# A fixed order on every engine, from a list schedule over all instructions, in a hybrid diffusion block

## The chip, the cores and the metric

The kernel runs on one core of one Trainium2 chip. The metric is the device time of one execution in microseconds. The core's engines have queues of their own: TensorE (PE; its weight loads are PEld), VectorE (DVE), ScalarE (ACT), GpSimd (POOL) and SyncE (SP, which here only issues transfers). Each queue is taken in its own order; an instruction whose inputs are not there holds all that stand behind it on the same queue.

## What is computed

Two layers over 256 context tokens and 512 latent tokens of width 1024, all in fp32. Layer 1 updates the latent tokens alone. Cut from the reference:

```python
mod_l = (jax.nn.silu(c) @ mod_w[i] + mod_b[i])[:, None, :]
sh1_l, sc1_l, g1_l, sh2_l, sc2_l, g2_l = jnp.split(mod_l, 6, -1)
p_lat = modulate(x_lat, sh1_l, sc1_l) @ w_in[i]
p_ctx = modulate(x_ctx, sh1_c, sc1_c) @ w_in[i]
y_ctx, y_lat = token_mixers(p_ctx, p_lat, ...)
x_lat = deepnorm_update(x_lat, y_lat @ w_out[i], g1_l, ln1_g[i], ln1_b[i])
m_lat = sq_relu_mlp(modulate(x_lat, sh2_l, sc2_l), w_up[i], w_down[i])
x_lat = deepnorm_update(x_lat, m_lat, g2_l, ln2_g[i], ln2_b[i])
```

The context has its own modulation, made from `c_ctx`, and in layer 0 the same two updates. The mixers, gMLP, grouped attention and gated DeltaNet, stand side by side. The DeltaNet runs in chunks of 64 tokens, forwards and backwards, and each chunk needs the inverse of a triangular matrix.

## The kernel before

**Staging.** A layer has four stages. `mix` first modulates the normed tokens and makes the projections for the gates and the gMLP; then it makes the nine convolution units (`dn_conv`), the queries and keys (`qk_norm`) and the values and `z`, while `dn_prep` works on the DeltaNet's decay matrices for two pairs of heads at a time. In its third part `dn_make` and `dn_scan` run for three pairs of heads beside `attention`. `rest` then multiplies the mixed tokens by `w_out` (`outp`, with `after` for norm and modulation) and calls `mlp`, which goes through the hidden width in eight groups of three to five 128-wide units: the up products of a group, squared ReLU, then the down products, token tile by token tile, into one PSUM tile (`ax`) of 1024 columns each; VectorE adds it to `acc`. Beside layer 0's MLP, `mod_dve` computes the next layer's modulation on VectorE, one step (`acc<-modw,cz,acc`) at each signal `pace`.

**Products.** Weights and activations are split into a high and a low fp32r part (`whi`, `wlo`; the split takes one ScalarE and one VectorE instruction), and each product is three (`mm3`). The DeltaNet's products are 64x64 or 32x32 and use a part of the array, so that two or four run side by side. `Feed` streams weights: `raw` buffers for the load (`wraw`), `parts` buffers for the split halves, five in the MLP.

**The inverse.** `dn_prep` transposes the masked matrix to `Lx` on VectorE, then runs 31 steps of two VectorE instructions (`tm`, then `Xx`), each on the result of the one before, and transposes the result to `PA` and `PB`.

**What sets the order.** `Flow` (line 40 on) runs the stages' generators while the program is written. It keeps a small clock of its own and always continues the one that could start earliest, with `BIAS` 1000 ns in favour of the DeltaNet's chains. It also hands out PSUM: four tiles `mm` of 512 columns and two tiles `ax` of 1024 are lent by name, so which product uses which tile, and in which turn, is fixed by then. The scheduler of the programming layer takes the finished text, in which each instruction has a priority by its place (`AHEAD` moves `dn_prep` 300 places forward), and puts out for each engine the ready instruction of the best priority. Every instruction goes through `_Engine.call`, line 213, which is why the profile puts all of them on L213 and one has to go by tile names. `_body` (line 656) builds and runs the kernel; `K.open` and `K.close` (line 302 on) open and close the SBUF pools, and a tile of a new pool waits for the tiles that lay in its place.

Of the kernel before, what the change touches and what calls it, by code (L numbers as in the profile page):

```python
# [9 lines left out]
F32R = mybir.dt.float32r  # L10
# [3 lines left out]
PSUM = bass.MemoryType.PSUM  # L14
DRAM = bass.MemoryType.DRAM

P = 128
# [22 lines left out]
class Flow:  # L40
# [8 lines left out]
    def __init__(self, tc):  # L49
        self.tc = tc  # L50
        self.free = {}
        self.ready = {}
        self.done = {}
        self.live = []
        self.count = 0
        self.last = 0.0
        self.slots = {}
        self.spare = {}
        self.lent = {}
# [7 lines left out]
    @staticmethod  # L67
    def width(a):
        n = 1
        for s in a.shape[1:]:  # L70
            n *= s
        return n
# [150 lines left out]
            setattr(self, k, _Engine(flow, k, getattr(nc, k)))  # L223


def _tb(v):

    return 1 - v if v < 2 else 7 - v
# [62 lines left out]
class K:  # L291
    def __init__(self, ctx, tc, d, dump=None):
        self.tc = tc
        self.flow = Flow(tc)
        self.nc = _Core(tc.nc, self.flow)
        self.d = d
        self.dump = dump
        self.ctx = ctx
        self.open_ = []


    def open(self, name, side="left", space=None):
        kw = {} if space is None else {"space": space}
        cm = self.tc.tile_pool(name=name, bufs=1, side=side, reuse_waits="tile", **kw)
        p = cm.__enter__()
        self.open_.append((p, cm))
        return p

    def close(self, *pools):
        for p in pools:  # L310
            i = next(i for i, (q, _) in enumerate(self.open_) if q is p)
            self.open_.pop(i)[1].__exit__(None, None, None)

    def setup(self):
        nc, tc, ctx, d = self.nc, self.tc, self.ctx, self.d
# [340 lines left out]
def _body(ctx, tc, d, out, dump=None, stop=None):  # L656
    K_ = Kernel(ctx, tc, d, dump)
    K_.run(out, stop)
    for p, cm in reversed(K_.open_):
        cm.__exit__(None, None, None)  # L660

# [17 lines left out]
class Kernel(K):  # L679
# [784 lines left out]
    def dn_make(self, l, p, v, qkv, G, A, TT, r):  # L1464
# [5 lines left out]
        kds, ks, egc, be, E = G["kds"], G["ks"], G["egc"], G["be"], G["E"]  # L1470
        hs = slice(2 * p, 2 * p + 2)
        td = (v, _tb(v))
        a0 = 0 if l == 0 else 2
        he = lambda a: a.rearrange("p t (h e) -> p t h e", e=HD)
# [59 lines left out]
    def dn_scan(self, l, p, v, A, r, S, o):  # L1534

        nc, sc = self.nc, self.dn
        need = l == 0 or v > 1
        a0 = 0 if l == 0 else 2
        td = (v, _tb(v))
        mm = nc.tensor.matmul  # L1540
        halves = [_half(f) for f in range(2)]
# [405 lines left out]
```

## Time and profile before

| | us |
|---|---|
| median of 3 runs | 2045.34 |
| lowest and highest | 2045.0, 2048.18 |
| the profiled execution | 2041.46 |
| its span, first to last instruction | 2039.7 |
| mean granted TensorE clock (1 is full speed) | 0.949 |

A page of the profile gives the busy time of each engine, a view of stretches gives the same for any part of the span, a view of waits tells how long an engine stood idle and whose instruction ended that, and a timeline lists instructions by their start, equal neighbours merged. In rows of the timeline and of groups, `out<-in` are tile names without buffer numbers, then shapes; in a group, `x80 | 101.0, 1280 | 8.5` is the count, the busy us, the mean ns of one, and the idle us of the engine just before them. TensorE's matmuls overlap in the pipeline, so the duration of one is longer than its share.

### The profile page before, as it was taken

How to read it: one execution, taken by the hardware profiler on the slowest of the kernel's cores; microseconds unless marked ns; L12 is line 12 of the kernel's file. 1: busy time of each engine (PE TensorE's matmuls, PEld its weight loads, DVE VectorE, ACT ScalarE, POOL GpSimd, SP SyncE). 2: the span in 40 equal slices, each digit the busy share in tenths (PEclk: the TensorE clock that was granted, in tenths of full speed). 3: DMA queues.
4: the chain of work that ended last, by engine and by line, in shares of the span. 5: the costliest groups of instructions: out<-in, count | busy, mean ns of one | idle time of the engine just before them, and what ended most of it. 6: DMA issues, size and time to landing. Idle time of an engine off the chain costs nothing.

```text
span 2039.7 us, 35034 instructions
## 1 busy us (share of the span) xinstructions
PE 1859.0 (91%) x14424; PEld 1508.4 (74%) x14424; DVE 1280.2 (63%) x2159; ACT 854.6 (42%) x1607; POOL 283.8 (14%) x479
## 2 busy tenths in 40 slices
PE   6999887888898999999999979988878879999997
PEld 2788665666678878887888777877667668788886
DVE  4668786856688154544555866879785585444555
ACT  3434434467546322331232174543655554323331
POOL 1111215531021000000000121121522020000001
PEclk8999898989999999999999979987998989999999
DMA  7211016213327223333453333110000554222331
GB/s 280 91 63 49 27 45 216 76 38 111 118 96 232 86 90 118 114 114 92 156 165 106 102 136 99 53 37 20 20 27 19 176 184 136 83 83 84 113 105 50
DMA packets 79172, 204.49 MB, mean 100 GB/s; under 512 B 15854, under 2 KB 30062, under 8 KB 77988
## 3 DMA queue, kind: packets, MB, share of 16 engines
q1 hardware_dynamic: 67876, 184.56, 28.0%
q10 hardware_dynamic: 11136, 17.70, 2.3%
q8 instruction: 113, 1.85, 0.4%
q14 instruction: 47, 0.39, 0.1%
HBM read 184.41 MB, written 17.82 MB: 99 GB/s over the span
## 4 chain that ended last, share of the span: by engine, by line
PE 61%; DVE 19%; issue 7%; ACT 5%; POOL 4%; DMA 4%; SPq 0%; ACTq 0%; POOLq 0%; DVEq 0%
PE mm L213 36%; PE ax L213 25%; DVE cacc L213 2%; DVE wlo L213 2%; DVE tm L213 2%; DVE Xx L213 2%; POOL crn L213 2%; DMA modw<-in_mod_w 1%; DVE M L213 1%; DMA wraw<-in_w_up 1%; POOL rs L213 1%; DVE st L213 1%; DMA wraw<-in_w_out 1%; ACT ape L213 1%; DVE anm L213 1%
## 5 line engine op out<-in xcount | busy, mean ns | idle before, releaser
L213 DVE TENSOR_TENSOR wlo<-wraw,whi 128x1024 fp32r<-128x1024 f32 (+2 forms) x188 | 226.5, 1211 | 254.8 <-ACT whi L213 254.4
L213 ACT ACTIVATE whi<-wraw 128x1024 fp32r<-128x1024 f32 (+2 forms) x188 | 194.5, 1049 | 450.7 <-PE ax L213 287.9
L213 PE MATMUL mm<-x2xh,whi 128*128 128x256 f32 (+1 forms) x832 | 287.8, 346 | 12.4 <-ACT whi L213 11.4
L213 PE MATMUL mm<-x2xh,wlo 128*128 128x256 f32 (+1 forms) x832 | 286.6, 345 | 1.0 <-DVE wlo L213 1.0
L213 PE MATMUL mm<-x2xl,whi 128*128 128x256 f32 (+1 forms) x832 | 287.0, 345 | 0.0
L213 PE MATMUL ax<-whi,hh 128*128 128x512 f32 x640 | 251.3, 393 | 0.0
L213 PE MATMUL ax<-whi,hl 128*128 128x512 f32 x640 | 249.6, 391 | 0.0
L213 PE MATMUL ax<-wlo,hh 128*128 128x512 f32 x640 | 249.5, 390 | 0.0
L213 PEld LDWEIGHTS mm<-x2xh,whi 128*128 128x128 f32 x832 | 158.6, 191 | 36.1 <-ACT whi L213 12.1
L213 PEld LDWEIGHTS mm<-x2xh,wlo 128*128 128x128 f32 x832 | 158.5, 191 | 22.3 <-DVE wlo L213 1.5
L213 PEld LDWEIGHTS mm<-x2xl,whi 128*128 128x128 f32 x832 | 158.8, 191 | 21.1 <-issue 0.8
L213 DVE TENSOR_TENSOR acc<-acc,ax 128x1024 f32<-128x1024 f32 x68 | 82.9, 1219 | 144.0 <-PE ax L213 144.0
L213 PEld LDWEIGHTS ax<-whi,hh 128*128 128x128 f32 x640 | 120.1, 188 | 33.7 <-ACT hh L213 6.1
L213 PEld LDWEIGHTS ax<-whi,hl 128*128 128x128 f32 x640 | 120.1, 188 | 30.7 <-issue 4.2
L213 PEld LDWEIGHTS ax<-wlo,hh 128*128 128x128 f32 x640 | 120.2, 188 | 26.3 <-issue 1.7
L213 POOL TENSOR_SCALAR rs<-mv 128x1 f32<-128x1 f32 x52 | 32.9, 632 | 702.7 <-DVE mv L213 701.5
L213 DVE SCALAR_TENSOR_TENSOR acc<-modw,cz,acc 128x1024 f32<-128x1024 f32 x80 | 101.0, 1280 | 8.5 <-DMA modw<-in_mod_w 4.4
L213 ACT ACTIVATE rl<-mm 128x256 f32<-128x256 f32 (+1 forms) x104 | 51.0, 491 | 131.5 <-PE mm L213 131.3
L213 POOL MEMSET acc<- 128x1024 f32 x10 | 9.5, 954 | 477.1 <-PE mm L213 477.1
L213 ACT ACTIVATE v<-mm,sh,sc 128x128 f32<-128x128 f32 x152 | 58.3, 462 | 29.4 <-PE mm L213 25.2
L213 DVE SCALAR_TENSOR_TENSOR cacc<-cb,cw,cacc 128x772 f32<-128x772 f32 (+1 forms) x72 | 69.9, 973 | 0.7 <-ACT cacc L213 0.2
L213 DVE TENSOR_REDUCE anm<-ax 128x1 f32<-128x768 f32 (+1 forms) x60 | 50.5, 847 | 31.3 <-PE ax L213 30.9
(255 smaller groups left out, 4104.0 us busy)
## 6 DMA issues: line engine op xcount, KB each, us to landing
modw<-in_mod_w SPq DMA_DIRECT2D x64, 512.0 KB
wraw<-in_w_up SPq DMA_DIRECT2D x64, 512.0 KB
wraw<-in_w_down SPq DMA_DIRECT2D x64, 512.0 KB
wraw<-in_w_ch SPq DMA_DIRECT2D x22, 512.0 KB
modw<-in_mod_w SPq DMA_DIRECT2D x32, 256.0 KB
modw<-in_mod_w SPq DMA_DIRECT2D x8, 1024.0 KB
wraw<-in_w_out SPq DMA_DIRECT2D x16, 512.0 KB
x_d<-xt ACTq DMA_DIRECT2D x16, 512.0 KB
```

The lines of the kernel that those rows point to most:

```text
L213: return f(*args, **kw)
```

## The change

After the program text is written, a new class `Order` reads all its instructions. `graph` finds the data dependences from the memory that each one reads and writes, keeps users of one PSUM tile in turn, and adds the waits that come from reused SBUF (for which `Pools` records when pools open and close). `costs` gives each instruction a duration from its kind, width and engine. `units` joins neighbouring products that use different parts of the array, when their kinds (the names of their tiles) agree. `tail` works out the longest chain of costs behind each instruction, and `schedule` simulates the five engines and one DMA bus: whichever engine is free first takes, of what is ready, the instruction with the longest chain. On TensorE, among the first 16, one of the same kind as the last counts as 5000 ns longer, and a part of the array that is still busy counts against. `apply` ties each instruction to the one before it on its engine, for order only. No instruction is added or altered. The core of the diff:

```diff
+class Order:
+    SAME, OTHER = 110.0, 220.0
+    LOOK, STICK, LATE, SWITCH = 16, 5000.0, 20.0, 250.0
...
+    def costs(self):
...
+            if kind == "InstDMACopy":
+                o = x.outs[0].bass_ap
+                self.moved[-1] = 4 * math.prod(int(c) for _, c in o.ap)
+                c = 330.0 if eng == E.SP else 60.0
+            elif kind == "InstMatmult":
+                n = width(x.outs[0])
+                m = width(x.ins[1])
+                if x.ins[1].dtype == F32R:
+                    c = max(35.0 + 0.58 * m, 0.4175 * n + 13.0)
+                else:
+                    c = (1.0 if x.is_transpose else 2.0) * max(0.42 * m, 0.835 * n + 2.0)
...
+            elif eng == E.DVE:
...
+                c = 70.0 + (50.0 * vec if n > 1 else 40.0) + n * (1.9 if kind == "InstStreamTranspose" else 0.53 if fast else 1.04)
+            elif eng == E.Activation:
+                c = 100.0 + 0.82 * n + (100.0 if len(x.outs) > 1 else 0.0) + (170.0 if vec > 1 else 0.0)
...
+    def units(self):
+        pe = [i for i in range(self.n) if self.cells[i]]
...
+            self.kind[i] = tuple(a.bass_ap.tensor.name.split("_")[0].rstrip("0123456789") for a in (*x.ins, *x.outs) if hasattr(a, "bass_ap"))
+            part = len(self.cells[i]) < 16
+            if unit and (not part or used & set(self.cells[i]) or any(newest(j) > unit[0] and j not in unit for j in self.pred[i]) or self.kind[i] != self.kind[unit[0]]):
+                close()
+                unit, used = [], set()
...
+    def tail(self):
...
+        for i in reversed(order):
+            c = self.dur[i] + (2200.0 + self.moved[i] / 340.0 if self.moved[i] else 0.0) if i < self.n else 0.0
+            far[i] = c + max((far[j] + self.lag(i, j) for j in succ[i]), default=0.0)
...
+    def schedule(self, key):
...
+            elif e == E.PE:
+                some = [heapq.heappop(avail[e]) for _ in range(min(len(avail[e]), self.LOOK))]
+                worth = lambda c: (c[0] - self.STICK * (self.kind[c[1]] == last) + self.LATE * max(0.0, max(cell[q] for q in self.cells[c[1]]) - t), c[1])
+                pick = min(some, key=worth)
...
+                i = pick[1]
+                queue = [k for k in self.unit.get(i, ()) if k != i]
+            else:
+                k, i = heapq.heappop(avail[e])
+            t = max(t, ready[i])
+            if self.cells[i]:
+                t = max([t] + [cell[c] + (self.SWITCH if kinds[c] != self.kind[i] and not self.round[i] else 0.0) for c in self.cells[i]])
...
+    def apply(self):
+        far = self.tail()
+        out = self.schedule([-f for f in far])
+        dep = mybir.DependencyInfo(mybir.DependencyClass.NoSync, mybir.DependencyReason.DATA)
+        for e, seq in out.items():
+            for a, b in zip(seq, seq[1:]):
+                self.tc.add_manual_dep(self.ins[b], self.ins[a].name, dep)
...
     def open(self, name, side="left", space=None):
         kw = {} if space is None else {"space": space}
         cm = self.tc.tile_pool(name=name, bufs=1, side=side, reuse_waits="tile", **kw)
-        p = cm.__enter__()
+        p = _Pool(self.pools, cm.__enter__(), side)
...
 def _body(ctx, tc, d, out, dump=None, stop=None):
     K_ = Kernel(ctx, tc, d, dump)
     K_.run(out, stop)
+    Order(tc, K_.pools).apply()
```

## Rows read from the trace of the kernel before

**Rows 1.** Head of the page: span; busy us, share, instructions by engine.

```profile
span 2039.7 us, 35034 instructions
...
PE 1859.0 (91%) x14424; PEld 1508.4 (74%) x14424; DVE 1280.2 (63%) x2159; ACT 854.6 (42%) x1607; POOL 283.8 (14%) x479
```

**Rows 2.** Stretches: length; PE, PEld, DVE, ACT, POOL busy us; clock; DMA share; GB/s.

```profile
0.00:55.00 55.00, 35.20 (x130) 14.46 (x130) 25.69 (x66) 22.38 (x37) 5.64 (x18) 0.88 0.80 281
55.00:305.00 250.00, 226.94 (x1589) 191.48 (x1589) 187.53 (x399) 104.62 (x166) 42.62 (x48) 0.93 0.16 51
305.00:460.00 155.00, 127.70 (x2842) 96.58 (x2840) 101.65 (x276) 81.83 (x242) 69.98 (x153) 0.90 0.33 110
460.00:640.00 180.00, 156.85 (x1048) 126.64 (x1049) 126.22 (x194) 105.10 (x234) 25.82 (x32) 0.97 0.38 129
640.00:1174.00 534.00, 534.00 (x2673) 439.15 (x2671) 284.44 (x267) 149.41 (x199) 15.82 (x20) 1.00 0.38 119
1174.00:1430.00 256.00, 224.43 (x1560) 189.62 (x1558) 199.02 (x425) 127.96 (x222) 51.99 (x70) 0.87 0.22 69
1430.00:1580.00 150.00, 123.50 (x2498) 101.12 (x2500) 102.42 (x256) 87.96 (x223) 50.27 (x110) 0.87 0.07 22
1580.00:1680.00 100.00, 80.92 (x530) 64.75 (x526) 69.09 (x102) 53.57 (x118) 14.30 (x22) 0.95 0.51 175
1680.00:2022.00 342.00, 341.99 (x1540) 278.79 (x1539) 173.61 (x168) 121.78 (x172) 3.67 (x4) 1.00 0.30 95
```

**Rows 3.** TensorE's waits over the whole span: us in total, times, longest.

```profile
PE mm L213 <- ACT whi L213: 20.2, 8, 5.6
PE mm L213 <- DVE axn L213: 12.9, 6, 4.6
...
PE ax L213 <- DVE PB L213: 10.1, 5, 2.7
PE mm L213 <- DVE wlo L213: 9.6, 12, 2.3
```

**Rows 4.** Two inverse runs, stretches of `tm` steps alone; then VectorE's timeline.

```profile
168.45:228.02 59.57, 21.00 (x62) 0.96 0.12 36
257.24:297.85 40.61, 21.02 (x62) 0.96 0.14 46
...
201.45 1.02 DVE L213 SCALAR_TENSOR_TENSOR cacc<-cb,cw,cacc 128x772 f32<-128x772 f32 x1
```

**Rows 5.** A group of the page; VectorE's timeline in layer 0's MLP.

```profile
L213 DVE SCALAR_TENSOR_TENSOR acc<-modw,cz,acc 128x1024 f32<-128x1024 f32 x80 | 101.0, 1280 | 8.5 <-DMA modw<-in_mod_w 4.4
...
857.38 1.22 DVE L213 TENSOR_TENSOR acc<-acc,ax 128x1024 f32<-128x1024 f32 x1
858.52 4.86 DVE L213 SCALAR_TENSOR_TENSOR acc<-modw,cz,acc 128x1024 f32<-128x1024 f32 x4
863.31 1.21 DVE L213 TENSOR_TENSOR acc<-acc,ax 128x1024 f32<-128x1024 f32 x1
```

**Rows 6.** Timeline of the kernel's end.

```profile
2029.04 0.39 PE L213 MATMUL ax<-whi,hl 128*128 128x512 f32 x1
2029.46 1.22 DVE L213 TENSOR_TENSOR acc<-acc,ax 128x1024 f32<-128x1024 f32 x1 [0.69 <-PE ax L213]
...
2034.29 1.28 DVE L213 SCALAR_TENSOR_TENSOR xt<-xt,rstd,lb 128x1024 f32<-128x1024 f32 x1 [0.72 <-POOL rstd L213]
```

**Rows 7.** The group of table loads on ScalarE, then ScalarE's timeline around one.

```profile
L213 ACT ACT_TABLE_LOAD x13 | 16.7, 1283 | 5.4 <-DVE gc L213 4.5 <-PEq L1939 0.7
...
1211.70 1.19 ACT L213 ACTIVATE xmxh<-v 128x512 fp32r<-128x512 f32 x2
1212.91 1.28 ACT L213 ACT_TABLE_LOAD   x1
1214.20 0.21 ACT L213 ACTIVATE ea<-ea 128x12 f32<-128x12 f32 x1
```

**Rows 8.** TensorE's timeline in layer 0's DeltaNet stage.

```profile
348.10 1.04 PE L213 MATMUL mm<-kv,TT 64*64 64x128 f32 x15
```

More of the change, by code (lines that the diff above doesn't have):

```diff
@@ new lines, with __init__, size, tile @@
+class Pools:
+    def __init__(self):
+        self.events = []
+class _Pool:
+    def __init__(self, pools, pool, side):
+        self.pools, self.pool, self.side, self.tags = pools, pool, side, {}
+        pools.events.append(("open", self))
+    def size(self):
+        return sum(b * n for b, n, _ in self.tags.values())
+    def tile(self, shape, dtype, tag=None, bufs=1, name=None):
+        kw = {} if tag is None else {"tag": tag}
+        t = self.pool.tile(shape, dtype, bufs=bufs, name=name, **kw)
+        tag = tag or name
+        n = 4 * math.prod(shape[1:])
+        n = -(-n // 32) * 32
+        b, k, names = self.tags.get(tag, (0, 0, []))
+        names.append(t.tensor.name if hasattr(t, "tensor") else t.name)
+        self.tags[tag] = max(b, n), max(k, bufs), names
+        return t
@@ L299, in __init__ @@
         self.open_ = []
+        self.pools = Pools()
     def open(self, name, side="left", space=None):
@@ L312, in close @@
             self.open_.pop(i)[1].__exit__(None, None, None)
+            self.pools.events.append(("close", p))
     def setup(self):
```

296 lines of the change are left out of this document (added).

## The prediction, made blind

> **What bounds the kernel now.** I read the head of the page first, then the stretches of busy time, then TensorE's own waits, and last single stretches of the timeline. The head [rows 1] has TensorE busy for 1859.0 of 2039.7 us, so 181 us are idle and no other engine is near its limit (VectorE 1280.2). The stretches [rows 2] show that this is an average over two kinds of stage. In the two MLP stages (640 to 1174 and 1680 to 2022) TensorE is busy for 534.0 of 534 and 341.99 of 342 us at a granted clock of 1.00: no order of instructions makes these 876 us shorter, it can only make them longer. In the stages of projections, DeltaNet, attention and output projection TensorE idles for 23.1 us (55:305), 27.3 (305:460), 23.2 (460:640), 31.6 (1174:1430), 26.5 (1430:1580) and 19.1 (1580:1680), in sum 150.8 us, and its clock is down: 0.87 to 0.97. Of the rest of the idle time 19.8 us lie in the first stretch, where the DMA engines move 281 GB/s, and the last 10 us behind the last product. No engine fills a mixed stage: the busiest, TensorE apart, is VectorE with 199.02 of 256 us in 1174:1430. So these stages are bound by chains that go from engine to engine, and by the order in which each engine takes their links.
>
> **What the change is, as the trace sees it.** No instruction is added, removed or altered; there is no new semaphore. What is new is that each of the five queues, SP's and POOL's included, gets one fixed order, from a list schedule whose priority is the longest chain of modelled costs behind an instruction. The order before came out of the same data dependences too, with the order of the program text as its priority. Two things stay frozen. Flow still hands out the six PSUM tiles (`mm0` to `mm3`, `ax0`, `ax1`) by name while the program is written, and users of one PSUM tile keep their order. And the SBUF pools keep their places, so a tile of a later stage still waits for those that lay there. What can change is how six chains of PSUM users are threaded against each other, and what VectorE, ScalarE, POOL and the DMA queues do first.
>
> **First term: waits that the order makes.** By what ended them, TensorE waited [rows 3] 20.2 us for `whi` and 9.6 for `wlo` (weights split late on ScalarE and VectorE), 12.9 for `axn` (normalised queries and keys) and 10.1 for `PB` (the end of the triangular inverse). I count these four as made by the order: these producers had their inputs earlier and stood behind other work. The inverse shows it best: its first run takes 59.6 us from `Lx` to `PA`, but its 62 `tm` and `Xx` steps take 21.0 us of VectorE [rows 4]; convolution taps of 1.02 us, such as the one at 201.45, stand between its steps. The next run takes 40.6 us for the same work. A priority by the longest chain puts these steps first. The rest of the idle time I leave to the data. So 20.2 + 9.6 + 12.9 + 10.1 = 52.8 us are the order's own, and I take 50 of the 150.8 us; the bounds are 0 (the same chains wait elsewhere) and 150.8.
>
> **Second term: the clock.** The chip grants one of two levels, 1.2 or 2.4 GHz, so a mean of 0.87 over 256 us says that 2 x 0.13 x 256 = 67 us ran at the lower one; over the six mixed stretches it is 35 + 31 + 11 + 67 + 39 + 10 = 193 us [rows 2], in which work took twice its time: at most 96 us. The level is low in stretches where TensorE idles between products and at 1.00 where it doesn't. With a third of the idle gone I take 10 us; the bounds are 96 and, if the new order spreads the products more thinly, -20.
>
> **Third term: what the MLP stages lose.** The schedule prefers, by 5000 ns of priority, a product of the same kind as the last one. In the MLP's second half two token tiles have their `ax` tile free at once, with equal chains behind them. So products of two token tiles will alternate and both tiles will end together. Now they go one after the other: the sums `acc<-acc,ax` on VectorE come 5.9 us apart (857.38, 863.31) and take 1.21 to 1.22 each, behind the next tile's products [rows 5]. Paired, both `ax` tiles are full at one moment, and TensorE needs other work for 1.22 us of sum and some 0.4 us of hand-over (an estimate: the last product begins at 2029.04 and the sum at 2029.46 [rows 6], and the way back to TensorE is of the same kind, each less the product's own run). There are 3 x 8 such ends in layer 0 and 2 x 8 in layer 1, 40 in all; the bounds are 0 and 40 x 1.6 = 64 us. Up products of the next group cover some of them, but the five buffers of `whi`/`wlo` hold four down units, which leaves one unit of cover in each group. I count one bare end in each of 16 groups, less some 40% as pairs fall out of step after the first: 16 x 1.6 x 0.6 = 15 us lost.
>
> **Fourth term: stage ends.** Paired tiles also end together before a norm. At the end of the kernel the last tile goes from its sum at 2029.46 to the end of its second scaling at 2034.29 + 1.28 in 6.1 us [rows 6]; another tile's share may come in front of it. The end of each of the two output projections is alike. I take 10 us in all, between 0 and 3 x 6.1 = 18.
>
> **Fifth term: ScalarE's tables.** There are 13 table loads of 1.283 us now, 16.7 us [rows 7], in the two stretches where Gelu stands beside Exp and Tanh. `Order.costs` prices an activation by its width alone, so nothing in the new order keeps the functions together. Up to 13 more would be 17 us of ScalarE, and in 1174:1430 it has 128 of 256 us to hide them in; I take 4, between 0 and 17. The Trainium skill ("ScalarE: Activation LUTs", What ACT_TABLE_LOAD costs) gives 2.66 us for each change of set, 1.283 of load and some 1.38 of drain; by that price the bound would be 35 us. The trace [rows 7] agrees on the load but shows no drain: the activation before ends at 1212.89, the load runs from 1212.91, and the next activation begins at 1214.20.
>
> **The queues.** SP issues loads as buffers come free; a load put ahead of its turn holds the loads behind it. I cost that at nothing in the MLP stages, where DMA is busy for 0.30 to 0.38, and include it in the bounds of the first term elsewhere. VectorE's modulation sums (`acc<-modw`, 80 of 1.280 us, 101.0 us [rows 5]) were paced by hand beside the MLP; now they fill any gap there. That costs nothing as long as an `ax` sum has 5 us to spare, and 1.28 us or more for an end of a pair that meets one.
>
> **The sum.** The profiled execution took 2041.46 us: a span of 2039.7 and 1.8 around it. 2041.5 - 50 - 10 + 15 + 10 + 4 = 2010.5. It lies 3.9 us under the median of the runs shown, 2045.34, so I forecast a median of 2014.4, 1.5% faster. The case's own range is 1980 to 2040.
>
> **The rivals.** *The chains gain more.* If two thirds of the idle time go (100 us) with 30 us of clock, and the pairs cost 10: 2041.5 - 120 + 3.9 = 1925. For it: VectorE's 102 of 155 and 102 of 150 us in the DeltaNet stages leave room for that. Against: there TensorE is busy for 128 and 124 us, mostly with small products that keep their order in PSUM.
> *The pairs cost more than the chains gain: slower.* The place is the second half of the MLP. A pair that ends while modulation sums run waits behind them; now up to four come in a row, 4.86 us [rows 5]. With two of them (2.56 us) ahead of a sum the 24 ends of layer 0 cost 4.2 us each, those of layer 1 1.6, in sum 126; two thirds of that is 83. With 25 us gained by the first term and 14 lost by the fourth and fifth: 2041.5 + 83 - 25 + 14 + 3.9 = 2117. Against the first two terms as forecast it decides from (50 + 10 - 14) / 40 = 1.2 us of idle TensorE at each of the 40 ends. For it: TensorE has no slack there at all. Against: sums now have priority over modulation where their chain is longer, and up products fill.
> *The mixed stages lose.* The preference for the same kind holds a step of the scan back behind a run such as the 15 `kv` products of 1.04 us [rows 8], by half of it if the step comes due anywhere in the run. The 72 steps of the scans (2 layers, 3 pairs of heads, 6 tiles, 2 halves) would then cost 72 x 0.52 = 37 us: 2041.5 + 37 - 25 + 14 + 3.9 = 2071, slower. It decides from 0.15 us a step.
> *It does next to nothing.* PSUM tiles handed out beforehand and the frozen pools leave the order much as it was: within 4 us of 2045.
>
> **How the numbers follow.** A measurement of this kernel tells about 0.2%, 4 us, from no change. The forecast has 0.43, more from the chains 0.12, the pairs 0.26, the mixed stages 0.11, no change 0.08. Faster is 0.55, the same 0.08, slower 0.37. Both signs hold much of the chance, so the range is wide: from 1940, which leaves out the better half of the first rival, to 2105, which takes in the pairs up to 12 us under their centre.
>
> **What would show it.** Right: the first inverse run well under 59.6 us, `whi` and `wlo` together under half of 29.8 us in TensorE's waits, the granted clock of 1174:1430 above 0.87. Third term: any idle TensorE in the MLP stages, ended by `acc` on VectorE; none would refute it. Fifth: the number of table loads beside 13. The forecast is wrong if TensorE's idle time outside the MLP stays at 150 us, or if the MLP stages grow by more than 50.

## The result, and the profile after

| | before | after |
|---|---|---|
| median | 2046.76 | 2065.39 |
| lowest and highest of 4 | 2045.0, 2051.8 | 2064.6, 2066.6 |
| profiled execution, its span | 2041.46, 2039.7 | 2066.6, 2064.8 |
| mean granted clock | 0.949 | 0.948 |

All times are in us. The ratio of after to before is 1.0087 with a 95% interval of 1.0068 to 1.0107: the changed kernel is 0.9% slower, where I had forecast 1.5% faster (2014.4 us). The first and second fence answer to [rows 1] and [rows 2]: the head of the page, then stretches of the span, cut where the stages end in the changed kernel (length; busy us of PE, PEld, DVE, ACT, POOL; clock; DMA share; GB/s).

```profile
span 2064.8 us, 35099 instructions
...
PE 1871.9 (91%) x14424; PEld 1515.1 (73%) x14424; DVE 1283.9 (62%) x2159; ACT 842.2 (41%) x1605; POOL 293.1 (14%) x479
```

```profile
55.00:278.00 223.00, 215.24 (x1496) 182.96 (x1495) 182.26 (x384) 99.54 (x157) 45.39 (x47) 0.98 0.18 59
278.00:463.00 185.00, 140.85 (x3008) 108.58 (x3006) 115.69 (x302) 91.15 (x258) 70.73 (x155) 0.88 0.26 87
463.00:640.00 177.00, 159.08 (x967) 124.94 (x968) 116.17 (x178) 96.59 (x219) 22.31 (x30) 0.94 0.34 117
640.00:1174.00 534.00, 526.75 (x2674) 439.15 (x2673) 280.01 (x266) 146.33 (x207) 12.73 (x18) 0.99 0.38 123
1174.00:1409.00 235.00, 210.82 (x1401) 179.64 (x1399) 184.03 (x377) 116.17 (x203) 51.68 (x56) 0.89 0.23 75
1409.00:1591.00 182.00, 151.08 (x2754) 117.69 (x2754) 134.12 (x322) 100.56 (x249) 62.25 (x129) 0.90 0.07 22
1591.00:1684.00 93.00, 68.37 (x368) 53.50 (x366) 56.87 (x83) 41.34 (x88) 13.06 (x18) 0.89 0.46 160
```

The first line is layer 0's projections: they end at 278 where they ended at 307.7, TensorE is idle for 7.8 us of them and its clock is 0.98 (0.93 in 55:305 before). The second line is the DeltaNet stage, with 44.2 us idle of 185; in 305:460 before it was 27.3 of 155. The six lines without the MLP (the fourth) leave 7.8 + 44.2 + 17.9 + 24.2 + 30.9 + 24.6 = 149.6 us idle, against 150.8 before: the idle time moved, and none of it went.

A table by stage shows where to. A stage's border is the end of its last product in the trace; "head" is the time from layer 0's last down product to layer 1's first convolution product, "out-projection" reaches from the last attention product to the first up product, with the gaps at both ends. Times are for the profiled executions; columns 4 to 7 are experiments below.

| stage | before | after | proj_only | no_switch | proj_mix | proj_nosw |
|---|---|---|---|---|---|---|
| L0 projections | 307.7 | 278.2 | 277.6 | 277.5 | 279.4 | 278.4 |
| L0 DeltaNet, attention | 224.2 | 256.2 | 235.1 | 236.1 | 256.6 | 235.4 |
| L0 out-projection | 85.1 | 78.3 | 85.1 | 77.8 | 84.7 | 85.1 |
| L0 MLP | 557.8 | 564.3 | 557.6 | 558.7 | 557.9 | 560.9 |
| head of L1 | 42.5 | 46.8 | 41.1 | 47.2 | 42.1 | 43.2 |
| L1 projections | 202.8 | 185.3 | 185.0 | 187.7 | 185.6 | 187.5 |
| L1 DeltaNet, attention | 186.3 | 201.5 | 199.7 | 198.6 | 201.7 | 200.5 |
| L1 out-projection | 59.4 | 74.1 | 60.9 | 71.0 | 63.1 | 60.8 |
| L1 MLP | 363.6 | 366.9 | 363.8 | 365.8 | 363.3 | 363.5 |
| tail | 10.3 | 13.2 | 9.9 | 13.2 | 9.9 | 9.9 |
| span | 2039.7 | 2064.8 | 2015.9 | 2033.6 | 2044.3 | 2025.2 |

From before to after the two projection stages win 29.5 + 17.5 = 47 us. The two DeltaNet and attention stages lose 32.0 + 15.2 = 47 us, as much. The rest, +6.5 and +3.3 in the MLPs, +4.3, +14.7 and +2.9 at the stage ends and -6.8 in layer 0's out-projection, is the 25 us by which the span grew.

These two 47 us are in part one and the same: work has crossed the border. Before, the second inverse of layer 0 was done in time for its 192 small products (96 of `PB,M`, 48 each of `PA,zs` and `zs,PA`) to run ahead of the last projection product; in the changed kernel and in the four experiments of the table they stand behind it. So a second border is of use, the first `kv` product, with which `dn_make` begins (times in us):

| | before | after | proj_only | no_switch | proj_mix | proj_nosw |
|---|---|---|---|---|---|---|
| L0, last projection to first `kv` | 8.0 | 21.1 | 18.9 | 18.8 | 21.1 | 18.8 |
| L0, first `kv` to last attention product | 216.2 | 235.1 | 216.2 | 217.3 | 235.5 | 216.7 |
| L1, last projection to first `kv` | 2.8 | 1.1 | 2.5 | 1.5 | 1.1 | 1.5 |
| L1, first `kv` to last attention product | 183.4 | 200.4 | 197.2 | 197.1 | 200.6 | 199.0 |

Counted to it, layer 0 gains 16.4 us ahead of it (it comes at 299.3 in place of 315.7) and loses 18.9 behind it; layer 1 gains 19.3, counted from its first convolution product, and loses 17.0.

The inverse did what the first term says. These are the stretches of its first two runs with its `tm` steps alone, as in [rows 4] (length; VectorE's busy us; clock; DMA share; GB/s):

```profile
158.10:200.50 42.40, 21.16 (x62) 0.96 0.15 50
253.50:289.10 35.60, 21.20 (x62) 0.89 0.23 87
```

The first run takes 42.4 us for the same 21 us of steps, where it took 59.6. The second runs from 253.5 to 289.1 where it ran from 257.24 to 297.85 [rows 4], so it ends only 8.8 us earlier, while the projections end 29.5 us earlier. And here are TensorE's waits over the span, to be read beside [rows 3] (us, times, longest):

```profile
PE mm L213 <- ACT whi L213: 19.8, 6, 9.3
...
PE mm L213 <- DVE rP L213: 13.1, 10, 3.0
...
PE mm L213 <- DVE S L213: 10.6, 12, 2.7
...
PE mm L213 <- DVE wlo L213: 7.9, 2, 7.4
...
PE mm L213 <- DVE axn L213: 5.7, 4, 2.3
```

Two of these rows in the kernel before:

```profile
PE mm L213 <- DVE rP L213: 11.5, 12, 2.2
...
PE mm L213 <- DVE S L213: 4.4, 7, 1.1
```

`axn` has more than halved, but `whi` and `wlo` stand at 27.7 us (29.8 before): 9.3 and 7.4 us of that are now single waits, ahead of layer 1's out-projection and in its head. `rP` and `S` are links of the scan: `rP`, third largest before, has grown a little, and `S` has more than doubled.

### The profile page after: what moved, and what is told of

Same layout as the page of the kernel before. It is cut to its first block, busy times and chain, and to the rows that moved or that the text cites. A ratio compares the mean times of both kernels' runs of the same rounds, so it can differ in the third digit from the quotient of the medians.

```text
span 2064.8 us, 35099 instructions
## 1 busy us (share of the span) xinstructions
PE 1871.9 (91%) x14424; PEld 1515.1 (73%) x14424; DVE 1283.9 (62%) x2159; ACT 842.2 (41%) x1605; POOL 293.1 (14%) x479
## 5 line engine op out<-in xcount | busy, mean ns | idle before, releaser
L213 PE MATMUL mm<-x2xh,whi 128*128 128x512 f32 (+1 forms) x832 | 212.1, 349 | 9.3 <-ACT whi L213 4.5
L213 PE MATMUL ax<-whi,hh 128*128 128x512 f32 x640 | 208.9, 395 | 6.4 <-ACT hh L213 3.6
L213 PE MATMUL mm<-x2xl,whi 128*128 128x256 f32 (+1 forms) x832 | 208.8, 346 | 0.0
L213 PE MATMUL mm<-x2xh,wlo 128*128 128x256 f32 (+1 forms) x832 | 207.2, 345 | 0.0
L213 PE MATMUL ax<-wlo,hh 128*128 128x512 f32 x640 | 206.3, 391 | 0.1
L213 PE MATMUL ax<-whi,hl 128*128 128x512 f32 x640 | 202.5, 391 | 0.2 <-DVE hl L213 0.2
L213 PEld LDWEIGHTS mm<-x2xl,whi 128*128 128x128 f32 x832 | 145.9, 192 | 21.1
L213 ACT ACTIVATE rl<-mm 128x512 f32<-128x512 f32 (+1 forms) x104 | 49.2, 495 | 106.6 <-PE mm L213 105.9
L213 DVE TENSOR_TENSOR hl<-rl,hh 128x768 fp32r<-128x768 f32 (+2 forms) x76 | 53.8, 716 | 46.3 <-ACT hh L213 46.1
L213 ACT ACTIVATE v<-mm,sh,sc 128x128 f32<-128x128 f32 x152 | 56.9, 468 | 38.5 <-PE mm L213 31.6
L213 PE MATMUL mm<-whi,yh 128*128 128x512 f32 x160 | 59.0, 405 | 14.9 <-ACT whi L213 11.1
```

The lines of the kernel that those rows point to most:

```text
L213: return f(*args, **kw)
```

## Experiments

Each kernel was timed in three rounds beside the kernel before on the same chip. A stage in what follows is a part of the program text: projections (A), DeltaNet and attention (C), out-projection (D), MLP (E), each with its layer; a list `self.stage` holds the part of each instruction. No experiment leaves out any computation.

### Which stages gain, which lose

Kernel `proj_only`:

```diff
         for e, seq in out.items():
+            seq = [i for i in seq if self.stage[i][0] == "A"]
             for a, b in zip(seq, seq[1:]):
```

> The fixed order is put only on instructions of the projection stages (modulation, gates, gMLP, convolutions, queries, keys, values, of both layers); all others are left to the old scheduler. In the changed kernel layer 0's projections end at 278.2 us where they ended at 307.7 (29.5 earlier), layer 1's take 11 us less, and the DeltaNet and attention stages behind them take 32 and 15 us more. Theory one, the new order inside the DeltaNet stages is what is bad: they go back to 224 and 186 us, the gain of 40 us is kept, 2046.8 - 40 = 2007. Theory two, the DeltaNet stages end when their own chains let them, however early the projections end: 2047, the same as before. A clear loss would say that the new order of the projections itself starts things late (2060 or more).

Measured: 2018.21, ratio 0.9877 (0.9857 to 0.9896). So the new order of the projections alone makes the kernel 1.2% faster than before. It keeps 24 of the 47 us: layer 0's DeltaNet stage takes 235.1 us, 21 less than in the changed kernel, but still 11 more than before, and layer 1's 199.7, about as much as in the changed kernel. Theory one holds for layer 0 to two thirds. The remainder there stands ahead of the first `kv` product, on TensorE's timeline, first in the kernel before and then in `proj_only`:

```profile
301.77 1.71 PE L213 MATMUL ax<-PB,M 32*32 32x32 f32 x96 [1.96 <-DVE PB L213]
...
315.75 2.79 PE L213 MATMUL mm<-kv,TT 64*64 64x128 f32 x22 [8.03 <-DVE kv L213]
```

```profile
290.54 2.77 PE L213 MATMUL ax<-PB,M 32*32 32x32 f32 x96 [12.94 <-DVE PB L213]
...
296.45 1.97 PE L213 MATMUL mm<-kv,TT 64*64 64x128 f32 x16
```

The projections are done at 277.6, and TensorE idles 12.94 us for the end of the second inverse and then runs its products; the kernel before had begun these products at 301.77, ahead of the end of its projections at 307.7, and behind that waited 8.0 us, for `kv`. From the first `kv` product on, the stage takes 216.2 us in both kernels. So layer 0 gains 19.3 us, the first `kv` product's, and keeps all of them; the other 10 of the 29.5 were work behind the border. Layer 1 keeps about 4 of its 17.8 us. There, too, work has crossed: 96 of VectorE's `tm` and `Xx` steps lie behind the projections in place of 62, and its busy time there is 138.3 us in place of 126.3. That this makes the loss is likely, not shown; TensorE's granted clock, 0.85 there in place of 0.90, is another candidate, but it is 0.91 in the changed kernel, whose layer 1 loses as much.

Kernel `no_mixers`, with the same line and the condition `self.stage[i][0] != "C"`:

> The fixed order is put on every stage but the DeltaNet and attention stages, which are left to the old scheduler. In the changed kernel the stages behind attention lose 7.5 us (start of layer 1's output projection), 6 (its end to the first up product), 3.3 (MLP of layer 1), 6.5 (MLP of layer 0) and 2.9 (the tail), less 3.4 won in layer 0's output projection: about 23. Theory one (the order inside the DeltaNet stages is bad): 2007 + 23 = 2030. Theory two (these stages end by their own chains): 2047 + 23 = 2070.

Measured: 2040.13, ratio 0.9972 (0.9955 to 0.9990). That is 22 us above `proj_only`: the new order of the output projections, the MLPs and the tail costs 22 us by itself. In the profiled executions most of the difference lies where it was expected, from layer 0's out-projection on; but 6 us of it lie ahead of that, in layer 0's DeltaNet stage (241.4 us), whose order is left to the old scheduler in both.

### Four suspects in the schedule

Kernel `no_kind`:

```diff
-    LOOK, STICK, LATE, SWITCH = 16, 5000.0, 20.0, 250.0
+    LOOK, STICK, LATE, SWITCH = 16, 0.0, 20.0, 250.0
```

> The changed kernel with the preference for a product of the same kind as the last one set from 5000 ns to 0. Theory A, this preference holds steps of the scan back behind runs of other products and pairs the token tiles in the MLP: DeltaNet stages of 230 and 190 us in place of 256 and 201, and the MLP of layer 0 back at 558 us from 564: 2065 - 26 - 11 - 6 = 2022. Theory B, the loss comes from the longest-chain priority and the transfers' order, not from the preference: 2060 to 2070. It can also be slower, if the runs of one kind saved time in the array's sharing: 2080 or more.

Measured: 2074.71, ratio 1.0154 (1.0133 to 1.0175): 9 us slower than the changed kernel. Layer 0's DeltaNet stage took 270.6 us. The preference for the same kind, which my third rival held guilty, is a gain there. One part of theory A came true: layer 0's MLP took 557.0 us, and layer 1's 360.6, so in these two stages the preference costs 7 and 6 us.

Kernel `sp_free`:

```diff
         for e, seq in out.items():
+            if e == mybir.EngineType.SP:
+                continue
```

> The changed kernel, but SyncE's queue of transfers gets no fixed order; the four computing engines do. In the changed kernel layer 1's output projection starts 9.3 us after the last attention product (1.8 before), because its weights are issued at 1611.19, behind loads of y that wait for attention's last store. Theory T, the transfers' order makes the losses at the stage ends: that gap goes back to about 2 us, the one to the first up product from 13 to 7, the tail from 13 to 10, 16 us in all: 2049. If the transfers' order only follows the rest, nothing changes: 2065.

Measured: 2079.15, ratio 1.0173 (1.0151 to 1.0196): 14 us slower than the changed kernel. The gap ahead of layer 1's output projection did shrink, from 9.3 to 4.0 us, but the other two stayed at 13 us, and both DeltaNet stages took 7 us more. A fixed order on the engines whose loads come in another order costs more than the fixed loads do.

Kernel `no_switch`:

```diff
-    LOOK, STICK, LATE, SWITCH = 16, 5000.0, 20.0, 250.0
+    LOOK, STICK, LATE, SWITCH = 16, 5000.0, 20.0, 0.0
```

> The changed kernel with the price of 250 ns for a product of another kind on the same part of the array set to 0. In the changed kernel the products `id,qd` and `A,rwu`, which alternate in the program by twos on the same two quarters of the array, lie spread out: from the end of `rwu` to the start of `rP` a tile of layer 0 takes 11.0 us in the mean where it took 5.2 before (5.1 with the order on the projections alone), and one run of them 3.4 us in place of 1.1. Theory S, the schedule believes that each change of kind costs 250 ns and puts other products between, which the scan then waits for: without the price 11.0 falls to 6 or less, the DeltaNet stages end some 20 and 10 us earlier, 2065 - 30 = 2035. Theory P, the priority by the longest chain itself is at fault: 2060 to 2070, and the 11 us stay.

Measured: 2036.12, ratio 0.9969 (0.9954 to 0.9984), as theory S expected: 29 us faster than the changed kernel through one constant, 20 of it in layer 0's DeltaNet stage. Layer 1's became only 3 us shorter, where 10 were expected; the rest came from layer 0's MLP and layer 1's out-projection. The time from `rwu` to `rP`, a mean over the 18 tiles of layer 0, fell from 11.0 to 7.3 us, short of the 6 expected. TensorE's waits for the links of the scan in 278:470 show it too, in the changed kernel and then without the price:

```profile
PE mm L213 <- DVE rP L213: 6.8, 6, 3.0
...
PE mm L213 <- DVE S L213: 5.3, 5, 2.7
...
PE mm L213 <- ACT rQ L213: 4.8, 3, 3.4
```

```profile
PE mm L213 <- DVE rP L213: 2.1, 4, 1.2
...
PE mm L213 <- ACT rQ L213: 1.9, 3, 1.3
...
PE mm L213 <- DVE S L213: 1.3, 2, 1.2
```

16.9 us have become 5.3. What the price does in the changed kernel is seen on TensorE's timeline of one tile, one of the slow ones. Its `rwu` was ready at 308.25, and this is the part from the first `id,qd` on:

```profile
323.55 0.27 PE L213 MATMUL mm<-id,qd 64*64 64x64 f32 x2
...
323.93 1.06 PE L213 MATMUL mm<-modw,cz 128*32 128x512 f32 x8
324.93 0.33 PE L213 MATMUL mm<-id,qd 64*64 64x64 f32 x4
...
325.97 0.28 PE L213 MATMUL mm<-A,rwu 64*64 64x64 f32 x4
326.08 0.28 PE L213 MATMUL mm<-id,qd 64*64 64x64 f32 x4
326.20 0.28 PE L213 MATMUL mm<-A,rwu 64*64 64x64 f32 x4
...
327.66 0.33 PE L213 MATMUL mm<-id,qd 64*64 64x64 f32 x4
327.92 1.06 PE L213 MATMUL mm<-modw,cz 128*32 128x512 f32 x8
328.92 0.33 PE L213 MATMUL mm<-A,rwu 64*64 64x64 f32 x4
```

`id,qd` and `A,rwu` alternate on the same two quarters of the array, and between them stand products of the modulation (`modw,cz`, 1.06 us each time) and others, so the run lasts from 323.55 to 329.25. `rP` waits for the end of it and starts at 329.37, 21 us after `rwu`. The run makes 5.7 of these; before it TensorE was at the tile ahead, whose own run lasted from 312.94 to 318.91. In `proj_only` the same kind of run looks like this:

```profile
426.40 0.28 PE L213 MATMUL mm<-id,qd 64*64 64x64 f32 x4
426.52 0.28 PE L213 MATMUL mm<-A,rwu 64*64 64x64 f32 x4
426.64 0.28 PE L213 MATMUL mm<-id,qd 64*64 64x64 f32 x4
...
426.75 0.28 PE L213 MATMUL mm<-A,rwu 64*64 64x64 f32 x4
...
427.22 0.28 PE L213 MATMUL mm<-A,rwu 64*64 64x64 f32 x4
...
427.62 0.42 DVE L213 TENSOR_TENSOR rP<-mm,ei 128x256 f32<-128x256 f32 x1 [0.90 <-PE mm L213]
```

Each change of kind takes 0.11 to 0.12 us, the groups' own run included; the schedule reckons 250 ns on top. By the single records, two products of one kind start 0.058 us apart on the same quarter (426.403 and 426.461), and the first of the next kind follows after 0.059 (426.520). One part of the expectation missed: the runs themselves stayed long, 2.9 us in the median (3.4 in the changed kernel, 1.1 before), so other products still stand in them without the price.

Kernel `any_units`:

```diff
-            if unit and (not part or used & set(self.cells[i]) or any(newest(j) > unit[0] and j not in unit for j in self.pred[i]) or self.kind[i] != self.kind[unit[0]]):
+            if unit and (not part or used & set(self.cells[i]) or any(newest(j) > unit[0] and j not in unit for j in self.pred[i])):
```

> The changed kernel, but neighbouring products that share the array are joined to a unit whatever their kinds. So `kd,rwu` and `rwu,kd`, which use different halves of the array's quarters, go side by side again: before, their 32 records took 0.69 us a tile, in the changed kernel 0.98. If their separation costs the scan its 0.3 us on each of 36 tiles: 2065 - 11 = 2054. If that is covered: 2065. The alternation of `id,qd` and `A,rwu` uses the same quarters and isn't joined by this, so the theory of the 250 ns price expects no more than the 11 us.

Measured: 2088.76, ratio 1.0225 (1.0200 to 1.0250): 23 us slower than the changed kernel, which neither line expected. The 32 records of `kd,rwu` and `rwu,kd` are back at 0.69 us a tile, but the same joining puts the scan's `S,rP` and `S,rQ` into one run (`S,rQ` some 1.6 us a tile in the median in place of some 0.8), and layer 1's DeltaNet stage takes 224.6 us. That the second made the loss is not shown, and one number speaks against it: `S,rQ` took 1.5 us a tile in the kernel before as well, whose DeltaNet stages are the shortest of these three. The cause of this loss stays open.

### The priority, and an order on some engines only

Kernel `text_key`:

```diff
-        out = self.schedule([-f for f in far])
+        out = self.schedule([float(i) for i in range(self.m)])
```

> The changed kernel, but the list schedule's priority is the place in the program text, as before the change, in place of the longest chain; costs, units, preference and the fixed order stay. If the longest-chain priority is at fault in the DeltaNet stages: about 2020 to 2045, and the gain in the projections (29.5 us in layer 0) shrinks too, since that priority made it. If the schedule's prices are at fault, or an order fixed by modelled times as such: 2065 or more, with `rwu` to `rP` still at 8 us or above.

Measured: 2075.65, ratio 1.0167 (1.0137 to 1.0196). The text's order as priority is 10 us worse than the longest chain. In its profiled execution (2083.55) both projection stages are longer (layer 0's end at 291.1, not at 278.2; layer 1's take 196.7 us, not 185.3), layer 0's out-projection too (89.8), while its MLP is shorter (551.3). Layer 0's DeltaNet stage is as slow as in the changed kernel (257.8 us). So the longest chain is not what slows it.

Kernel `mix_nope`:

```diff
         for e, seq in out.items():
+            seq = [i for i in seq if self.stage[i][0] == "A" or self.stage[i][0] == "C" and e != mybir.EngineType.PE]
             for a, b in zip(seq, seq[1:]):
```

> The fixed order on the projections for all engines, and in the DeltaNet and attention stages for all engines but TensorE; the rest is left to the old scheduler. With the projections alone it was 2018.2. If TensorE's order is what makes the DeltaNet stages slow: 2015 to 2022, the same. If VectorE's, ScalarE's, GpSimd's or SyncE's order is: 2018 + 20 + 3 (what the changed kernel loses there in the two layers) = 2041.

Measured: 2087.64, ratio 1.0223 (1.0194 to 1.0252). Layer 0's DeltaNet stage took 287.7 us, more than with either full order. With TensorE in one order and its suppliers in another the question can't be answered; the run shows that the order of one engine has no price of its own.

### Stage ends, and a kernel put together

Kernel `ends_free`, the price at 0 and the condition `self.stage[i] not in ("D1", "E1")`:

> The price of another kind at 0, and the fixed order on everything but the output projection and the MLP of layer 1 with the tail, which are left to the old scheduler. In the kernel without the price these took 11.6 + 2.2 + 2.9 = 16.7 us more than before (last attention product to first up product 71.0 in place of 59.4, MLP 365.8 in place of 363.6, tail 13.2 in place of 10.3). If the order at the stage ends makes that (two token tiles reach their norms together, weights stand behind y loads): 2036 - 17 = 2019. If the lateness comes in from the attention stage before: 2036.

Measured: 2022.65, ratio 0.9887 (0.9869 to 0.9904), 13.5 under `no_switch`. The stretch from the last attention product to the first up product went from 71.0 to 61.0 us, the MLP from 365.8 to 363.6, the tail from 13.3 to 9.9. In the changed kernel the first of these gaps reads as follows, on the queues and on TensorE:

```profile
1608.36 1.74 SPq L213 DMA_DIRECT2D y<-y_d  x2
...
1610.90 0.33 ACTq L213 DMA_DIRECT2D y_d<-ayb  x1
1611.19 5.98 SPq L213 DMA_DIRECT2D wraw<-in_w_out  x3
...
1618.77 1.06 ACT L213 ACTIVATE whi<-wraw 128x1024 fp32r<-128x1024 f32 x1 [3.54 <-DMA wraw<-in_w_out]
...
1619.88 1.22 PE L213 MATMUL mm<-whi,yh 128*128 128x512 f32 x2 [9.31 <-ACT whi L213]
```

The last three weights of the projection are issued at 1611.19, behind loads of `y` that were put ahead of them on SP, and TensorE waits 9.31 us (1.8 in the kernel before). The tail shows the other kind of end, two token tiles together, on VectorE:

```profile
2050.26 1.22 DVE L213 TENSOR_TENSOR acc<-acc,ax 128x1024 f32<-128x1024 f32 x1 [3.29 <-PE ax L213]
...
2052.12 1.20 DVE L213 TENSOR_TENSOR acc<-acc,ax 128x1024 f32<-128x1024 f32 x1
...
2058.45 2.48 DVE L213 SCALAR_TENSOR_TENSOR xt<-xt,rstd,lb 128x1024 f32<-128x1024 f32 x2 [0.71 <-POOL rstd L213]
```

From the last sum at 2052.12 to the end of the second scaling at 2060.93 it takes 8.8 us, where [rows 6] has 6.1 for one tile.

Kernel `best`, the price at 0 and the condition `self.stage[i] in ("A0", "C0", "D0", "A1", "C1")`:

> The price of another kind at 0, and the fixed order on the projections, the DeltaNet and attention stages of both layers and the output projection of layer 0; the two MLPs, layer 1's output projection and the tail are left to the old scheduler. From the stages measured so far: with the order on the projections alone it was 2018.2; layer 0's output projection with its gaps took 77.8 us in place of 85.1 in the kernel without the price. So 2018 - 7 = 2011, if stages add up. If the change of order at a border between the two schedulers costs something, 2018 or more.

Measured: 2036.14, ratio 0.9950 (0.9935 to 0.9965), 25 above the sum of its stages. Layer 0's MLP behind the border took 571.0 us, 13 more than before. There TensorE waits 5.6 us for `wlo` and 4.1 for `whi` in 595:660, and the first down product starts 51.7 us after the first up product (39 in `proj_only`). Stages don't simply add: the border between two orders has a price here, and the name of the kernel was premature.

Kernels `no_late` (the third constant, the penalty for busy parts, at 0 as well) and `best_late` (the same on the stages of `best`):

> The changed kernel with the price of another kind at 0 and also the penalty on a product whose part of the array is still busy (20 ns of priority for each ns) at 0. Without the price alone the runs of `id,qd` and `A,rwu` were still 2.9 us long in the median (1.1 before). If this penalty is what keeps them apart: 1.5 us or less, and the DeltaNet stages shorter by up to 10 us each: 2036 - 15 = 2021. If the remaining length comes from inputs that arrive late: 2036, no change.

> Both prices at 0, and the fixed order on the same stages as in the run with the price of another kind at 0 (projections, DeltaNet and attention, layer 0's output projection). If the penalty on busy parts matters it lies 10 to 15 us below that run, near 1998; if not, level with it at 2011.

Measured: 2041.89, ratio 0.9984 (0.9971 to 0.9997), and 2035.64, ratio 0.9955 (0.9940 to 0.9969). The penalty neither makes the remaining loss nor keeps the runs apart (2.7 us in the median). Layer 0's DeltaNet stage took 239.0 us in both.

### Does the price act in the DeltaNet stages, and by itself?

`proj_mix` has the condition `self.stage[i][0] in "AC"` and the changed kernel's prices, `proj_nosw` the same with the price of another kind at 0.

> The fixed order of the changed kernel, its prices as they are, on the projections and on the DeltaNet and attention stages of both layers; output projections, MLPs and tail are left to the old scheduler. With the projections alone it was 2018.2. If the order of the DeltaNet stages is what gives the gain back: layer 0's stage 256 us in place of 235.1, layer 1's 201.5 in place of 199.7, so 2018 + 23 = 2041, unless the border to the old scheduler adds to it (the run with layer 0's output projection in the new order lost 13 us in the MLP behind its border). If the loss needs the new order in the later stages too: near 2018.

> The same stages, projections and DeltaNet with attention, with the price of another kind at 0. If that price is what makes the DeltaNet stages slow: layer 0's stage 236 us and layer 1's 199, as with the old scheduler, so 2018 to 2022 and some 20 under the run with the price. If the price acts elsewhere: level with it.

Measured: 2046.68, ratio 1.0013 (1.0001 to 1.0025), and 2026.76, ratio 0.9911 (0.9895 to 0.9927). The price costs 20 us with the later stages left alone, and the table has them in one row: layer 0's DeltaNet stage takes 256.6 us with it and 235.4 without, as long as under the old scheduler (235.1). `proj_nosw` lies 5 us above what was expected of it and 8.5 above `proj_only`; why is open.

Kernel `text_nosw`, the text's order as priority and the price at 0:

> The order on all stages with the price of another kind at 0, and the place in the program text as the priority in place of the longest chain. With the price, the text's order gave 2075.7 against 2065.4 for the longest chain. If price and priority are separate causes, the price takes off its 29 us here too: 2046, and the longest chain is worth 10. If the price only hurts together with the longest chain: 2070 or more.

Measured: 2052.97, ratio 1.0044 (1.0029 to 1.0059): 23 us under `text_key`, though 7 above what was expected. Layer 0's DeltaNet stage went from 257.8 to 237.0 us, layer 1's from 205.4 to 192.7. The price acts by itself, under either priority.

The fastest kernel measured is `proj_only` at 2018.2, ahead of before (2045) and of the changed kernel (2065).

## Why the prediction was wrong

The sign was wrong. That 2065 lies within the range of 1940 to 2105 is due to the range, which was wide enough to hold the rivals.

**First term (-50): right in kind, too large, and then given back.** The projections became 47 us shorter, and the mechanism named is there: the first inverse and `axn` come earlier. But the four waits that I had added up to 52.8 us still make 38.5 (19.8, 7.9, 5.7 and, for `PB`, 5.1), and `rP`, with 11.5 us the third largest wait of that view, stood outside my sum: a wait of the very stage that then lost. Part of the 47 us is work that crossed the border. Counted to the first `kv` product the gain is 16.4 + 19.3 = 36 us. Two signs that I gave fit (the first inverse run at 42.4 us; the granted clock of 1174:1430 at 0.89, a little above the 0.87 of [rows 2]). Two spoke against it and were right: `whi` and `wlo` stayed at 27.7 us, and the idle time outside the MLP at 149.6. `proj_only` shows that even under the old scheduler only 24 of the 47 us reach the end: 19 from layer 0, where all that the first `kv` product gained is kept, and 4 from layer 1.

**The step that failed: the DeltaNet stages had no term.** I wrote that the rest of the idle time I leave to the data, and so costed the new order there at nothing. It cost 32.0 and 15.2 us. The third rival names the place and nearly the time (2071 against 2065), but I gave it 0.11 and blamed the preference for the same kind. `no_kind` refutes that. The cause in layer 0 is the price of 250 ns for another kind on the same part of the array, shown by `no_switch`, by `proj_mix` against `proj_nosw` and by `text_nosw` against `text_key`: from the first `kv` product on, layer 0's stage takes 235.1 us in the changed kernel, 216.2 before, and 217.3 and 216.7 without the price; under the text's order as priority it takes 233.2 with the price and 217.2 without. So the price makes all but 1 us of the loss there. That the rival's 2071 came near is luck: its 37 us stood for the preference. I had this constant before me in the diff and held it to no row. The trace of before could have refuted it, since there a run of `id,qd` and `A,rwu` with its changes takes 1.1 us in the median. The remaining 11 to 13 us of layer 0's stage stand ahead of the first `kv` product: the later end of the second inverse and its products, which before ran beside the projections. In layer 1 some 14 us from the first `kv` product on stand in `proj_only` too, under the old order of that stage. It stays open what makes them, as does why the runs of `id,qd` and `A,rwu` are still long without the price.

**Second term (-10, clock): nothing.** The mean granted clock is 0.948, before 0.949. It rose in the projections (0.98) and fell at the out-projection of layer 1: 0.89 in 1591:1684, 0.95 in 1580:1680 before.

**Third term (+15, pairs in the MLP): the pairs came, their cost didn't.** Before, no sum `acc<-acc,ax` started within 1.4 us of the one ahead of it; in the changed kernel 29 of 68 did. On VectorE's timeline such a pair is one row:

```profile
744.77 2.35 DVE L213 TENSOR_TENSOR acc<-acc,ax 128x1024 f32<-128x1024 f32 x2 [5.07 <-PE ax L213]
```

TensorE's waits in layer 0's MLP (616:1177) hold these two rows:

```profile
PE mm L213 <- ACT whi L213: 4.2, 2, 3.3
...
PE ax L213 <- ACT acc L213: 0.7, 1, 0.7
```

In layer 1's MLP (1685:2052) one wait was ended by VectorE's sum:

```profile
PE ax L213 <- DVE acc L213: 1.1, 1, 1.1
```

So no more than 0.7 + 1.1 us was lost to sums. Layer 0's MLP grew by 6.5 us through other things: TensorE idles 9.5 us in it (1.3 before), longest for weights split late, and 21 transposes `c_ident,xn` that ran ahead of its first up product before now run in it. Against that stands a gain that I had held impossible ("no order of instructions makes these 876 us shorter"). The modulation's 40 products `acc,ones`, each on a quarter of the array's columns, ran in 17 short runs before and run in 7 now; `units` joins such products. One run in the kernel before, then one in the changed kernel:

```profile
716.71 1.05 PE L213 MATMUL mm<-acc,ones 128*32 128x512 f32 x2
```

```profile
715.61 1.06 PE L213 MATMUL mm<-acc,ones 128*32 128x512 f32 x8
```

That is worth some 10 us, 10 runs of 1.0; in `text_nosw`, where less idle time stands against it, layer 0's MLP took 546.7 us, 11 less than before. `no_switch` has 28 pairs of sums and an MLP of 558.7 us, 0.9 above before. Nor does the preference make them: `no_kind` has 30. The second rival, which lived on this term, falls with it.

**Fourth term (+10, stage ends): right kind, a little small.** The head of layer 1, its out-projection and the tail lost 4.3 + 14.7 + 2.9 = 21.9 us, and layer 0's out-projection won 6.8 (in part by the transposes that now run in the MLP), so 15. `ends_free` takes back 13.3 of it, in the kernel without the price: 10.0 at the out-projection and 3.3 at the tail. Half of the largest part is not tiles that end together but weights behind `y` on SP, which I had left to the bounds of the first term, without a price ("a load put ahead of its turn holds the loads behind it" was the right sentence).

**Fifth term (+4, tables): the wrong sign.** There are fewer loads, not more:

```profile
L213 ACT ACT_TABLE_LOAD x11 | 14.1, 1283 | 2.9 <-DVE gpo L213 2.0 <-PEq L2349 0.7
```

Against the sum: -50, -10, +15, +10, +4 were -47, 0, +10, +15 and -3 at the most, which would have come to 2017. The term that was missing is +47 by the table's borders; counted from the first `kv` product it is +36, beside a first term of -36.

## What to carry to other kernels

A list schedule is a set of prices, and it puts work wherever a price says an engine will be idle; so hold each constant against a row of the trace, above all those that say two instructions can't follow each other closely, before judging the priority rule. Judge an order stage by stage: measure it on one stage with the rest left as it was. And before a stage's gain is booked, look whether the same work still stands ahead of its border: of the 29.5 us that layer 0's projections won, 10 were work that now runs behind them. An order belongs to all queues at once: to fix some of them, or to stop at a border where loads for the next stage are already in flight, can cost more than either full order.

## What the runs showed of the hardware

Products of 64x64 of different kinds alternate on the same quarters of the array at 0.11 to 0.12 us a group of four records, with nothing lost at the change (0.058 us from start to start within a kind, 0.059 across, in `proj_only`), and 32 records on all four quarters take 0.69 us. Products on a quarter of the columns (128*32) take as long for eight records side by side, 1.06 us, as for two, 1.05. Sums of 1.2 us on VectorE, 29 of 68 of them back to back with the one ahead, cost TensorE no more than 1.8 us in the two MLPs of 564 and 367 us; I had reckoned with 1.6 us for every bare pair.
